# A decoder layer with 32 experts: the first two experts chosen from the counts of two token tiles, and another order of the experts

## The chip, the core and the metric

The kernel runs on one core of a Trainium2 chip. The metric is the device time of one execution in microseconds (us). TensorE is called PE, VectorE DVE, ScalarE ACT, GpSimd POOL and SyncE SP; SP issues nearly all transfers from HBM. "Tile" has three senses here, so they are kept apart: a *token tile* is 128 of the 512 tokens, a *weight tile* is one transfer of 1 MB of expert weights (1.0486 million bytes), and a *slot* is the SBUF buffer that a weight tile lands in.

## What is computed

One layer: an attention mixer, a layer norm, then 32 experts of which each token takes four, and a second layer norm. Cut to what matters:

```python
x = layer_norm(DN_ALPHA * x + mixed, ln1_g, ln1_b)            # 512 x 1024
logits = (xt @ w_router + b_router); top_logit, top_idx = lax.top_k(logits, 4)
gates = softmax(top_logit)
# for each expert e, over the tokens that chose it:
h = xb @ w_gate_up[e] + b_gate_up[e]                          # 1024 -> 2048
act = (clip(up, -7, 7) + 1) * (min(gate, 7) * sigmoid(1.702 * gate))
y = act @ w_down[e] + b_down[e]                               # 1024 -> 1024
out[token] += gate_of(token, e) * y
x = layer_norm(DN_ALPHA * x + out, ln2_g, ln2_b)
```

Everything is float32. An expert's weights are 12 MB, 8 weight tiles of gate/up and 4 of down; all 32 are read, 402.7 million bytes.

## The kernel before

**Attention** works by token tile, in the order 0, 3, 1, 2 (`ORDER`); `PLAN` starts one head's scores per step and carries out one task of a finished token tile in between: `mix_all`, `out_proj` twice, `norm`, `logits`, `logits2`, `ranks`. `route` picks the four experts of each token, `rank` counts for each token its place among the tokens of its expert. After the last token tile `counts` adds up the tokens per expert, and `order_experts` sorts the experts into the *positions* of `KINDS`, the largest counts into the roomiest kinds.

**Kinds.** A position of kind H has 128 places and multiplies in three passes of split weights: ACT writes the high part (L251), DVE the low part (L252), into *hi/lo rooms* (three `whi`, three `wlo` of 1 MB each). Kind L has 64 places and T has 32; both take the raw float32 weights as they landed, with 2 or 4 row groups of PE at a time (L1377). G is H and T at once, D is H and L at once. A slot comes free when an H tile has been split, or when the last matmul on a raw tile is done.

**The stream.** `Stream.ahead` (L153) issues weight tiles on SP in a fixed order whenever a slot is free: 11 slots (`NRAW`) during attention, some of them lent to q, k, v, 12 in the expert stage. `hold` stops it until `order_experts` is done, since until then no expert's number is known. Position 0 is an exception: it is always expert 0, so its 12 weight tiles can be fetched during attention (the `order` list brings its down tiles ahead of position 1's). The w_o weights sit split in the hi/lo rooms and two slots until the last `out_proj`.

**The first token rows.** While the last token tile is in hand, the rows of expert 0 from the other three are gathered (`prep2`, `gather`); the last token tile's rows come by matmuls with a selection (`first_xT`, L1270). In the stage itself PE runs gate/up of position b and then down of position b-1; `between(k)` prepares the next positions. At the end `tail` reads the outputs back and does the second layer norm.

Of the kernel before, what the change touches and what calls it, by code (L numbers as in the profile page):

```python
# [9 lines left out]
F32 = mybir.dt.float32  # L10
F32R = mybir.dt.float32r
BF = mybir.dt.bfloat16
# [30 lines left out]
KINDS = "HTLHLLGLTHLHLLDLTHLHHTHLHLHHHLLL"  # L43
# [6 lines left out]
assert len(KINDS) == E and KINDS[:2] == "HT" and KINDS[-3:] == "LLL"  # L50
# [47 lines left out]
def constants():  # L98
# [30 lines left out]
    by_room = [0] + sorted(range(1, E), key=lambda b: -CAP[KINDS[b]])  # L129
# [4 lines left out]
    put("keys", np.broadcast_to(np.where(np.arange(E) < 1, 2.0 ** 21, 0) + E - 1 - np.arange(E), (P, E)))  # L134
# [5 lines left out]
class Stream:  # L140


    def __init__(self, kn):
        self.kn, self.src, self.raw, self.cv = kn, [], {}, {}
        self.nd = self.nc = self.at = 0

        self.order, self.hold = None, 1 << 30
# [5 lines left out]
    def ahead(self, most=None):  # L153
        kn = self.kn
        while self.nd < min(len(self.src), self.hold) and kn.used < kn.limit and (most is None or self.nd <= most):
            i = self.order[self.nd] if self.order else self.nd
# [51 lines left out]
class Kernel:  # L208
# [14 lines left out]
    def raw_slot(self, dt=F32):  # L223

        j = self.free.pop(0)
# [4 lines left out]
    def release(self, *tiles):  # L230
        for t in tiles:
            j, = [j for j, s in self.slots.items() if s is t]
            del self.slots[j]
            self.free.append(j)

    def release_all(self):
        self.slots, self.free = {}, list(range(self.nslots))
# [64 lines left out]
    def setup(self, ctx):  # L302
# [32 lines left out]

        order = list(range(len(self.st.src)))
        order[n0 + 8:n0 + 20] = order[n0 + 16:n0 + 20] + order[n0 + 8:n0 + 16]
        self.st.order, self.st.hold = order, n0 + 12
# [254 lines left out]
    def attention(self):  # L593
        nc, tc, i = self.nc, self.tc, self.i
        with ExitStack() as cx:
# [157 lines left out]
            ranked = []  # L753

            def norm(q):
# [6 lines left out]
                if len(ranked) == NT - 1:  # L762
                    self.xT0 = [sc.tile([P, 512], F32, name="xT0", tag="sc") for _ in range(2)]
                    self.first_xT(self.xg[0], self.ident, True)

            def logits(q):
# [19 lines left out]
                nc.sync.dma_start(self.x1d[q * P:(q + 1) * P], z)  # L786
# [8 lines left out]

            def ranks(q):
                self.rank(q)
                ranked.append(q)
                if len(ranked) < NT:
                    self.places(q)  # L800
                    self.prep_tile((0, 0), q)
                else:
                    mf = w.tile([P, P], F32, name="mf1", tag="pT", bufs=3)
                    nc.vector.tensor_scalar(mf, self.iob, self.rk1[:, q, 0:1], None, op0=ALU.is_equal)
                    ps = self.counts()
                    x1 = state.pop((q, "z"))
                    self.first_xT(x1, mf, False, range(4))
# [969 lines left out]
```

## Time and profile before

| | |
|---|---|
| median of 3 runs | 1383.42 us (1383.14 to 1383.57) |
| the profiled execution | 1382.91 us, of which the span of instructions 1381.0 |
| mean granted TensorE clock | 0.967 of full speed |
| PE / DVE / ACT / POOL busy | 91% / 53% / 40% / 12% |
| moved by DMA | 464.69 MB, on average 336 GB/s |
| chain that ended last, by engine | PE 43%, DMA 39%, DVE 8% |

The profile's page cuts the span into 40 slices of 34.5 us; attention and routing are the first nine or so, the expert stage the rest. A matmul's busy time is longer than its spacing, since matmuls are pipelined. Times in the views count from the first instruction.

### The profile page before, as it was taken

The page shows a single profiled execution, that of the slowest core. Times are in us where ns is not written, and L with a number is a line of the kernel's source. Part 1 is how long each engine was busy: PE and PEld are TensorE (multiplying, and loading weights), DVE is VectorE, ACT ScalarE, POOL GpSimd, SP SyncE. Part 2 cuts the span into 40 slices and gives each one's busy share as a digit, 9 for nine tenths or more (in the row PEclk, how much of TensorE's full clock was granted, in tenths as well). Part 3 has the DMA queues.
Part 4 walks back from the last instruction along what each step waited for, and adds up shares of the span by engine and source line. Part 5 has one row for each costly group of instructions (what it writes and reads, how often), then busy time and mean ns, then how long its engine had stood idle before and what let it go on. Part 6 is the DMA issues. An engine that isn't in the chain of part 4 may idle for free.

```text
span 1381.0 us, 17825 instructions
## 1 busy us (share of the span) xinstructions
PE 1256.8 (91%) x6424; PEld 804.6 (58%) x6424; DVE 734.4 (53%) x1280; ACT 559.2 (40%) x828; POOL 160.4 (12%) x180
## 2 busy tenths in 40 slices
PE   6989698978999899998999999999998999999972
PEld 5768597866564354555544445477574657875320
DVE  4553555458563254356434336288565567973155
ACT  3432543324352143335234235267444365753201
POOL 2232100011010000101000001010010110000004
PEclk9999899887999999999999999999999999999987
DMA  9201641348999999999999999999999999999981
GB/s 331 86 1 61 240 146 62 122 157 298 374 418 420 419 419 419 417 419 418 421 418 420 363 394 386 418 419 418 420 418 419 419 419 409 418 387 419 415 363 71
DMA packets 76331, 464.69 MB, mean 336 GB/s; under 512 B 10306, under 2 KB 11506, under 8 KB 26064
## 3 DMA queue, kind: packets, MB, share of 16 engines
q1 hardware_dynamic: 65824, 435.42, 77.3%
q0 software_dynamic: 7840, 18.66, 3.7%
q10 hardware_dynamic: 2576, 9.44, 1.9%
q8 instruction: 52, 0.85, 0.2%
q14 instruction: 39, 0.32, 0.1%
HBM read 445.60 MB, written 25.03 MB: 341 GB/s over the span
## 4 chain that ended last, share of the span: by engine, by line
PE 43%; DMA 39%; DVE 8%; ACT 3%; POOL 2%; issue 2%; ACTq 0%; SPq 0%; POOLq 0%; DVEq 0%
DMA raw<-in_w_gate_up_dram 23%; DMA raw<-in_w_down_dram 12%; PE acc L1377 10%; PE acc L258 6%; PE acc L259 6%; PE acc L260 6%; DVE wlo L252 3%; DMA yr<-yd 1%; DMA raw<-yd 1%; PE ip L258 1%; PE ip L260 1%; PE ip L259 1%; PE zp L260 1%; PE zp L258 1%; PE zp L259 1%
## 5 line engine op out<-in xcount | busy, mean ns | idle before, releaser
L252 DVE TENSOR_TENSOR wlo<-raw,whi 128x1024 fp32r<-128x1024 f32 (+3 forms) x361 | 422.1, 1222 | 136.3 <-ACT whi L251 133.6
L251 ACT CAST whi<-raw 128x1024 fp32r<-128x1024 f32 (+3 forms) x361 | 358.7, 1046 | 167.7 <-DMA raw<-in_w_down_dram 78.2
L1377 PE MATMUL acc<-raw,xTs 128*64 128x512 f32 (+1 forms) x1280 | 264.0, 600 | 11.7 <-DMA raw<-in_w_gate_up_dram 11.3
L258 PE MATMUL acc<-whi,xTh 128*128 128x512 f32 x448 | 182.8, 408 | 4.5 <-issue 3.9
L259 PE MATMUL acc<-wlo,xTh 128*128 128x512 f32 x448 | 177.9, 397 | 0.9 <-DVE wlo L252 0.9
L260 PE MATMUL acc<-whi,xTl 128*128 128x512 f32 x448 | 177.8, 397 | 0.0
L1377 PEld LDWEIGHTS acc<-raw,xTs 128*64 128x64 f32 (+1 forms) x1280 | 70.0, 129 | 146.0 <-issue 110.2
L1488 POOL DMA_INDIRECT yd<-y,idx x34 | 50.6, 1489 | 658.5 <-ACT y L1477 470.8
L1377 PE MATMUL acc<-raw,aTs 128*64 128x512 f32 (+1 forms) x704 | 115.5, 521 | 0.1
L1427 DVE TENSOR_SCALAR u<-acc 128x512 f32<-128x512 f32 (+1 forms) x48 | 31.8, 662 | 148.3 <-ACT s L1426 148.3
L258 PEld LDWEIGHTS acc<-whi,xTh 128*128 128x128 f32 x448 | 84.8, 189 | 36.4 <-issue 12.8
L259 PE MATMUL acc<-wlo,aTh 128*128 128x512 f32 x224 | 90.5, 404 | 13.6 <-DVE wlo L252 13.6
L259 PEld LDWEIGHTS acc<-wlo,xTh 128*128 128x128 f32 x448 | 84.8, 189 | 21.1 <-DVE wlo L252 2.7
L260 PEld LDWEIGHTS acc<-whi,xTl 128*128 128x128 f32 x448 | 84.7, 189 | 20.5
L258 PE MATMUL acc<-whi,aTh 128*128 128x512 f32 x224 | 90.1, 402 | 2.3 <-ACT whi L251 2.3
L1426 ACT ACTIVATE s<-acc 128x512 f32<-128x512 f32 (+1 forms) x48 | 27.5, 574 | 156.6 <-PE acc L1370 82.4
L260 PE MATMUL acc<-whi,aTl 128*128 128x512 f32 x224 | 88.8, 396 | 0.0
L1377 PEld LDWEIGHTS acc<-raw,aTs 128*64 128x64 f32 (+1 forms) x704 | 39.4, 128 | 66.8 <-issue 58.8
L1333 DVE SCALAR_TENSOR_TENSOR aTl<-tp,aTh 128x512 fp32r<-128x512 f32 x28 | 18.0, 686 | 106.6 <-ACT aTh L1329 106.6
L1305 POOL DMA_INDIRECT xg<-x1d,idx x34 | 40.3, 1185 | 294.5 <-issue 211.8
L1477 ACT COPY y<-acc 128x1024 f32<-128x1024 f32 (+2 forms) x32 | 23.6, 738 | 115.8 <-PE acc L260 61.4
L259 PEld LDWEIGHTS acc<-wlo,aTh 128*128 128x128 f32 x224 | 42.2, 188 | 29.5 <-DVE wlo L252 20.4
(333 smaller groups left out, 1533.6 us busy)
## 6 DMA issues: line engine op xcount, KB each, us to landing
raw<-in_w_gate_up_dram SPq DMA_DIRECT2D x256, 1024.0 KB, 20.4
raw<-in_w_down_dram SPq DMA_DIRECT2D x128, 1024.0 KB, 20.8
yd<-xg ACTq DMA_DIRECT2D x4, 2048.0 KB, 7.7
raw<-in_w_in_dram SPq DMA_DIRECT2D x6, 1024.0 KB, 15.1
raw<-yd SPq DMA_DIRECT2D x5, 1024.0 KB, 19.9
raw<-in_w_o_dram SPq DMA_DIRECT2D x4, 1024.0 KB, 5.0
yr<-yd SPq DMA_DIRECT2D x3, 1024.0 KB, 19.9
raw<-in_x_dram SPq DMA_DIRECT2D x4, 512.0 KB, 10.1
```

The costliest lines, as they stand in the source:

```text
L251: nc.scalar.copy(hi[:, js], t[:, js])
L252: nc.vector.tensor_tensor(lo[:, js], t[:, js], hi[:, js].bitcast(F32), op=ALU.subtract)
L258: nc.tensor.matmul(out, l[0], r[0], start=start, stop=False)
L259: nc.tensor.matmul(out, l[0], r[1], start=False, stop=False)
L260: nc.tensor.matmul(out, l[1], r[0], start=False, stop=stop)
L1305: nc.gpsimd.indirect_dma_start(out=B["xg"], out_offset=None, in_=self.rows(self.x1d, n), in_offset=bass.IndirectOffsetOnAxis(ap=B["idx"][: ...
L1333: nc.vector.scalar_tensor_tensor(lo, v, scale, hi.bitcast(F32), op0=ALU.mult, op1=ALU.subtract)
L1377: self.nc.tensor.matmul(o[n * i:n * i + n], lT, r, start=start, stop=stop)
L1426: nc.scalar.activation(s, ps[:, :w], AF.Silu, scale=SW)
L1427: nc.vector.tensor_scalar(u, ps[:, w:2 * w], LIM + 1.0, 1.0 - LIM, op0=ALU.min, op1=ALU.max)
L1477: nc.scalar.copy(y, B["d"])
L1488: self.nc.gpsimd.indirect_dma_start(out=self.rows(self.yd, n), out_offset=bass.IndirectOffsetOnAxis(ap=B["idx"][:, 1:2], axis=0), in_=y, i ...
```

## The change

1. **Two experts picked early.** When two token tiles are routed (0 and 3), `pick_first` takes the two experts with the fewest tokens so far; `keys` later forces them to positions 0 and 1. Both positions are now kind T. Their 16 gate/up tiles and the first one's down tiles (`hold = n0 + 20`) may then be issued; the experts' numbers are read by SP into registers. Nothing is fetched before that.
2. **Raw weights in rooms of split ones.** After w_o's last use the rooms that held it are taken by five weight tiles of position 1 (`extra`) and by the expert biases (`bias_early`, which now loads both).
3. **The last token tile's chain** is written out in `last_two`: the mixing of the last tile stands between the routing steps of the one before, no weights are split there, and the rows of the first expert for the last two token tiles come by matmuls of 32 columns (`first_rows`, `first_more`).
4. **Another order of positions**: 11 H and 15 L instead of 12 and 14; T, G and D as many as before.

```diff
-KINDS = "HTLHLLGLTHLHLLDLTHLHHTHLHLHHHLLL"
+KINDS = "TTLHHHLLLGTLDTLHHLLHLHLHHLLHHLLL"
...
     def ahead(self, most=None):
...
+            if kn.used >= kn.limit and not kn.extra:
+                break
...
     def raw_slot(self, dt=F32):
+        if self.extra:
+            tag = self.extra.pop(0)
+            t = self.hp.tile([P, 2048], dt, name="raw", tag=tag)
...
-        order[n0 + 8:n0 + 20] = order[n0 + 16:n0 + 20] + order[n0 + 8:n0 + 16]
-        self.st.order, self.st.hold = order, n0 + 12
+        self.n0 = self.st.hold = n0
...
             def ranks(q):
                 self.rank(q)
                 ranked.append(q)
-                if len(ranked) < NT:
-                    self.places(q)
-                    self.prep_tile((0, 0), q)
...
+                self.places(q)
+                self.route2(q)
+                if len(ranked) == 2:
+                    self.pick_first(ranked)
+                    self.st.hold = self.n0 + 20
                     self.st.ahead()
+                    B = self.blk[0, 0] = {}
+                    self.at0 = self.columns(B, 0, w)
+                    for t in ranked:
+                        self.prep_tile((0, 0), t)
                     self.prep2((0, 0), ranked)
                     self.gather((0, 0))
+            def last_two(p, q):
+                flush()
+                logits2(p)
+                mix_t(q, 1)
+                out_half(q, 1, 0)
+                self.rank(p)
+                ranked.append(p)
+                self.places(p)
+                mp = first_col(p)
+                self.route2(p)
+                out_proj(q, 0)
+                out_proj(q, 1)
+                for j in range(4):
+                    self.st.cv.pop(wo0 + j)
+                self.release(*self.in_ring)
+                self.bias_early(nc.scalar)
+                self.extra = ["whi", "wlo", "whi", "wlo", "whi"]
+                self.st.ahead()
+                flush()
+                norm(q)
+                self.xT0 = sc.tile([P, 512], F32, name="xT0", tag="sc")
+                self.first_rows(self.xg[0])
+                self.first_more(state.pop((p, "z")), mp, False)
+                logits(q)
+                logits2(q)
+                self.rank(q)
+                ranked.append(q)
+                ps = self.counts()
+                mq = first_col(q)
+                self.first_more(state.pop((q, "z")), mq, True)
+                self.order_experts(ps)
+                self.st.hold = len(self.st.src)
+                self.st.ahead()
+                self.places(q)
...
+    def pick_first(self, tiles):
+        ps = self.tp()
+        for j, t in enumerate(tiles):
+            nc.tensor.matmul(ps[:, :E], self.oneb, self.sel[:, t], start=j == 0, stop=j == len(tiles) - 1)
+        few = sm.tile([P, E], F32, name="few", tag="lg")
+        nc.vector.scalar_tensor_tensor(few, ps[:, :E], -float(E), self.c["iotae"], op0=ALU.mult, op1=ALU.add)
+        nc.vector.max(mx, few)
+        nc.vector.max_index(ix, mx, few)
+        nc.vector.tensor_copy(self.idf, ix[:, :2])
+        nc.vector.tensor_copy(self.ids, self.idf[:1])
...
+    def first_more(self, rows, mf, last):
+        for k in range(KD):
+            c = k % 2 * P + k // 2 * 32
+            self.nc.tensor.matmul(self.xT0[:, c:c + 32], rows[:, k * P:(k + 1) * P], mf, start=False,
+                                  stop=last and k == KD - 1)
```

The order of instructions shows the change at three places. On SP, from the write of the second token tile's rows (`x1d`) on; `z` is a token tile's input rows, `raw` a weight tile. Before:

```order
L786 DMA x1d<-z 128x1024
L710 DMA z<-in_x_dram 128x1024
L163 DMA raw_2173<-in_w_gate_up_dram 128x2048
L163 DMA raw_2175<-in_w_gate_up_dram 128x2048
L163 DMA raw_2177<-in_w_gate_up_dram 128x2048
L786 DMA x1d<-z 128x1024
L163 DMA raw_2331<-in_w_gate_up_dram 128x2048
L163 DMA raw_2333<-in_w_gate_up_dram 128x2048
L163 DMA raw_2335<-in_w_down_dram 128x2048
L710 DMA z<-in_x_dram 128x1024
L786 DMA x1d<-z 128x1024
```

and in the changed kernel:

```order
L788 DMA x1d<-z 128x1024
L1611 TENSOR_LOAD ids
L1611 ISA x2
L165 ISA
L165 DMA raw_2088<-in_w_gate_up_dram 128x2048
L165 ISA
L165 DMA raw_2099<-in_w_gate_up_dram 128x2048
L165 ISA
L165 DMA raw_2101<-in_w_gate_up_dram 128x2048
L715 DMA z<-in_x_dram 128x1024 x2
L165 ISA
L165 DMA raw_2222<-in_w_gate_up_dram 128x2048
```

Three weight tiles had been issued before these rows; now the load of the two numbers (`ids`) and the first three weight tiles stand ahead of the `z` loads, which both come here. After the next `x1d` write three more weight tiles follow, then the five in the rooms and two in w_o's slots.

On PE, from the rank of token tile 3 (`utb`) on, before:

```order
L996 MATMUL tp<-sel,utb 128x32
L684 MATMUL po<-raw_804,pT 128x128
L684 MATMUL po<-raw_807,pT 128x128
L684 MATMUL po<-raw_810,pT 128x128
L684 MATMUL po<-raw_474,pT 128x128
```

and in the changed kernel:

```order
L1020 MATMUL tp<-sel,utb 128x32
L1211 LDWEIGHTS oneb
L1211 MATMUL tp<-sel,oneb 128x32
L1211 LDWEIGHTS oneb
L1211 MATMUL tp<-sel,oneb 128x32
L1356 LDWEIGHTS m
L1356 MATMUL tp<-orh,m 128x4
L1356 LDWEIGHTS m
L1356 MATMUL tp<-orh,m 128x4
L689 MATMUL po<-raw_804,pT 128x128
```

The matmuls of the pick (L1211) and of the first expert's row numbers (L1356, which need DVE's `m`) now stand ahead of attention's.

On PE after the router logits of token tile 1 (`x1T`), before:

```order
L792 MATMUL tp<-wr,x1T 128x32 x8
L995 LDWEIGHTS oneb
L995 MATMUL tp<-sel,oneb 128x32
L995 LDWEIGHTS oneb
L995 MATMUL tp<-sel,oneb 128x32
L996 LDWEIGHTS utb
L996 MATMUL tp<-sel,utb 128x32
L1280 LDWEIGHTS m
L1280 MATMUL tp<-rh,m 128x4
```

and in the changed kernel:

```order
L794 MATMUL tp<-wr,x1T 128x32 x8
L722 MATMUL tp<-cst,mix 128x128 x4
L266 MATMUL zp<-whi,mh 128x512
L267 MATMUL zp<-wlo,mh 128x512
L268 MATMUL zp<-whi,ml 128x512
```

Twelve output-projection matmuls of token tile 2 (`zp`) now follow at once, then the rank of token tile 1, then the other 24; the three matmuls on `m` (L1280) are gone from here.

## Rows read from the trace of the kernel before

**Rows 1.** The page, 40 slices of the span: GB/s moved.
```profile
GB/s 331 86 1 61 240 146 62 122 157 298 374 418 420 419 419 419 417 419 418 421 418 420 363 394 386 418 419 418 420 418 419 419 419 409 418 387 419 415 363 71
```

**Rows 2.** Busy time by stretch: us, engines' busy us (instructions), clock, DMA share, GB/s.
```profile
280.00:300.00 20.00, 16.13 (x85) 13.21 (x84) 9.29 (x27) 2.58 (x6) 2.84 (x3) 0.83 0.57 222
300.00:320.00 20.00, 11.60 (x75) 10.15 (x73) 15.33 (x45) 7.44 (x14) 1.70 (x2) 0.74 0.51 188
320.00:340.00 20.00, 18.60 (x77) 14.30 (x78) 16.86 (x42) 11.18 (x15) 4.53 (x7) 0.83 0.79 275
340.00:360.00 20.00, 19.18 (x142) 11.18 (x140) 13.62 (x30) 9.46 (x13) 3.06 (x3) 1.00 0.85 330
360.00:380.00 20.00, 20.00 (x92) 12.06 (x92) 8.78 (x17) 6.51 (x9) 1.02 (x1) 1.00 1.02 419
...
770.00:790.00 20.00, 20.00 (x87) 9.40 (x89) 5.13 (x12) 2.28 (x4) 0.00 (x0) 1.00 0.84 331
820.00:840.00 20.00, 20.00 (x139) 9.25 (x139) 1.45 (x6) 3.43 (x6) 1.20 (x2) 1.00 0.85 321
1230.00:1250.00 20.00, 20.00 (x97) 10.69 (x97) 8.28 (x17) 7.50 (x9) 2.31 (x2) 1.00 0.92 366
```

**Rows 3.** Timeline of SP's issues: start us, us until the last, what, count.
```profile
263.38 1.29 SPq L163 DMA_DIRECT2D raw<-in_w_gate_up_dram  x3
...
285.00 1.21 SPq L163 DMA_DIRECT2D raw<-in_w_gate_up_dram  x2
286.26 0.49 SPq L163 DMA_DIRECT2D raw<-in_w_down_dram  x1
286.79 0.56 SPq L710 DMA_DIRECT2D z<-in_x_dram  x1
...
307.50 2.52 SPq L163 DMA_DIRECT2D raw<-in_w_down_dram  x3
318.92 42.02 SPq L163 DMA_DIRECT2D raw<-in_w_gate_up_dram  x16
```

**Rows 4.** Timeline of PE from 255 to 322 us; in brackets the idle time before.
```profile
255.02 0.18 PE L996 MATMUL tp<-sel,utb 128*128 128x32 bf16 x1
...
287.93 0.18 PE L996 MATMUL tp<-sel,utb 128*128 128x32 bf16 x1 [1.76 <-DVE sel L987]
...
289.38 0.19 PE L1280 MATMUL tp<-rh,m 128*128 128x4 bf16 x1 [1.24 <-DVE m L1246]
...
292.22 0.63 PE L260 MATMUL zp<-whi,ml 128*128 128x512 f32 x1
...
301.86 1.95 PE L1270 MATMUL xT<-cst,xg 128*128 128x128 f32 x16
...
321.40 0.76 PE L258 MATMUL acc<-whi,xTh 128*128 128x512 f32 x1 [3.86 <-issue]
```

**Rows 5.** Timeline of DVE, the same columns.
```profile
257.58 0.23 DVE L983 TENSOR_SCALAR gates<-gates,gs 128x4 f32<-128x4 f32 x1
...
270.34 0.69 DVE L747 SCALAR_TENSOR_TENSOR z<-z,zp 128x512 f32<-128x512 f32 x1 [0.16 <-PE zp L260]
...
298.01 0.69 DVE L747 SCALAR_TENSOR_TENSOR z<-z,zp 128x512 f32<-128x512 f32 x1 [6.14 <-DMA z<-in_x_dram]
...
307.17 3.70 DVE L252 TENSOR_TENSOR wlo<-raw,whi 128x512 fp32r<-128x512 f32 x6
...
315.93 0.17 DVE L1138 CAST vi<-v 1x32 int32<-1x32 f32 x1
...
325.32 0.29 DVE L1160 TENSOR_TENSOR otmp<-rk,oat 128x128 f32<-128x128 f32 x1
```

**Rows 6.** Matmul groups of a gate/up half: a T position, then an L position.
```profile
L1377 PE MATMUL acc<-raw,xTs 128*32 128x512 f32 x64 | 7.5, 597 | 0.0
...
L1377 PE MATMUL acc<-raw,xTs 128*64 128x512 f32 x64 | 14.6, 597 | 0.0
```

**Rows 7.** SP's waits between 765 and 860 us: total us, times, longest.
```profile
SPq L163 <- PE acc L1377: 55.2, 26, 5.8
```

More of the change, by code (lines that the diff above doesn't have):

```diff
@@ L233, in release @@
             del self.slots[j]
-            self.free.append(j)
+            if isinstance(j, int):
+                self.free.append(j)
     def release_all(self):
-        self.slots, self.free = {}, list(range(self.nslots))
+        self.slots, self.free, self.extra = {}, list(range(self.nslots)), []
     def convert(self, t, a, n, in_ring):
@@ L1032, in moe @@
         self.oh = mp.tile([P, 2, E], F32, name="oh")
-        xT = self.blk[0, 0]["xT"] = self.pair("xT")
-        for g in range(2):
-            self.split([x[:, 4 * g:4 * g + 4] for x in xT], self.xT0[g].rearrange("p (k t) -> p k t", k=4))
+        xT = mp.tile([P, 2, 4, 32], F32, name="xTs", tag="xTh")
+        nc.scalar.copy(xT, self.xT0[:, :256].rearrange("p (k h s) -> p k h s", k=2, h=4))
         self.rest()
+        self.bias_part(0)
         self.scx.close()
@@ new lines, in second_between @@
+        def second_between(k):
+            if k == 0:
+                next(perm)
+                self.prep_sel(1)
+            elif k == 1:
+                next(perm)
+                self.bias_part(1)
+            elif k == 2:
+                for _ in perm:
+                    pass
+                self.prep((2, 0))
+            elif k == 3:
+                self.prep2((2, 0))
+                self.gather((2, 0))
+            elif k == 4:
+                self.prep((3, 0))
+            elif k == 5:
+                self.load_aT(0)
+            elif k == 6:
+                self.prep2((3, 0))
+                self.gather((3, 0))
@@ L1265, in prep_sel, with first_rows @@
                 self.nc.vector.tensor_scalar(B["sel"][j], self.oneb, oh[j], None, op0=ALU.mult)
-    def first_xT(self, rows, mf, start, ks=range(KD)):
-        for k in ks:
-            self.nc.tensor.matmul(self.xT0[k // 4][:, k % 4 * P:(k % 4 + 1) * P], rows[:, k * P:(k + 1) * P], mf,
-                                  start=start and k % 4 == 0, stop=not start and k % 4 == 3)
+    def first_rows(self, rows):
+        for k in range(2):
+            self.nc.tensor.matmul(self.xT0[:, k * P:(k + 1) * P], rows[:, k * P:(k + 1) * P], self.ident,
+                                  start=k == 0, stop=False)
+    def first_more(self, rows, mf, last):
[3 more added lines that the diff above has]
+                                  stop=last and k == KD - 1)
     def prep2(self, u, tiles=range(NT)):
```

211 lines of the change are left out of this document (100 added, 111 removed).

## The prediction

> **What bounds the kernel now.** I read the page's slices first. From the twelfth slice on the transfers move 409 to 421 GB/s nearly throughout, until the last two; the eleven before move less, most of them far less [rows 1]. So the expert stage is a stream that can't go faster, about 419 GB/s or 2.50 us per weight tile of 1.0486 MB, and its end is set by two things: how many bytes have moved when the stream begins to flow, and how many are lost when it stops. Three places later on fall short, slices 23 to 25 and 36 [rows 1].
>
> I then read stretches, to price the shortfalls [rows 2]. From 300 to 360 us they are 419 - 188, 419 - 275 and 419 - 330 GB/s over 20 us each: 464 x 20 us = 9.28 MB. In the stage, 770 to 790 us lacks 88 x 20 us = 1.76 MB, 820 to 840 us 1.96 MB, 1230 to 1250 us 1.06 MB. PE is busy all through the last three: there the stream stops because all slots are full, and SP waits for PE's matmuls on raw tiles, 55.2 us in 26 waits [rows 7]. The first two lie at the D position, the third behind the three H in a row at positions 26 to 28.
>
> Why the start is slow: SP's issues are sparse. Three weight tiles have gone before those rows, six more by 286.7 us, three at 307.5; the thirteenth goes at 318.92 us, and the following sixteen take 42.0 us, since each waits for a slot [rows 3]. Between 287 and 307 us there is no free slot that may be filled, after 307 no expert that may be fetched. PE starts the experts at 321.40 us [rows 4], with an H position, which gives a slot back only as fast as splitting runs.
>
> Order on PE before that: logits of token tile 1, a wait of 1.76 us for the selection and 1.24 us for `m`, then 36 output-projection matmuls, which begin at half clock, 1.2 GHz (0.63 us for a matmul), and end near 302 us, where the row matmuls begin [rows 4].
>
> **The change, part by part.**
>
> *The pick (a new wait).* After the rank of token tile 3, PE has the matmuls on `m` ahead of attention's. DVE must first finish the gates, at 257.81 us [rows 5], then 17 small operations: the pick, the keys, the columns, two `m`. Such operations take 0.16 to 0.29 us [rows 5]; at 0.22 that is 3.8 us, so `m` is there near 261.6. PE, free at 255.20 [rows 4], idles 6.4 us; everything behind it on PE (scores, values, output projection of tile 1) and on DVE moves by that. The wait is new in kind; its ends are 3 us (DVE interleaves) and 10 us. I also charge 3 us for the clock: after the 1.8 and 1.2 us waits at 288 us the granted clock was 0.83 of full in that stretch, so 17% of 20 us was lost [rows 2], and an idle spell of 6 us will not do better.
>
> *SP.* The two numbers are ready near 258.7, and SP had its first weight tile out 2.8 us after `vi` was written [rows 3, 5], so the first three tiles go at about 261.5 to 263.5. The three tiles fetched earlier than that before are no loss: the engines are nearly idle there. The `z` loads now stand behind three weight tiles. In the same position `z` of tile 2 was issued at 286.79 and arrived after 298.01 [rows 3, 5], 11.2 us; that puts `z` of tile 1 at 275, and DVE took it at 270.34 before [rows 5] and now comes 6.4 us later, near 277. I price it at nothing; without that cover it costs up to 4 us. The second three tiles follow as before, the third three wait behind the `x1d` write of tile 1 and go near 293 instead of 285.
>
> *The last tiles.* The waits of 1.76 and 1.24 us and the 3.4 us of lower clock go, because twelve matmuls of tile 2 stand there: 6.4 us, just what the pick costs. The projection so ends at 302 + 3 (clock) = 305. Behind it, DVE's splitting of 3.70 us no longer stands before the logits (2.9 us of it were in their way), and the 3.86 us before the first expert matmul shrink to one copy [rows 4, 5]: the experts start near 321.4 + 3 - 2.9 - 3 = 318.5.
>
> *The rooms (the main gain).* Counting from 293 us: three tiles and an `x1d` write, three tiles into rooms whose last use is over near 299, biases of 0.8 MB, two tiles in rooms and two in slots from 305, one in the twelfth slot: 11 tiles and 1.3 MB, 12.8 MB or 31 us of transfers. That reaches to 324, and slots come back from 319.5 on, one per 0.94 us, since a T half has 7.5 us of matmuls on 8 tiles [rows 6], against 2.50 us per transfer. So the flow is unbroken from 293 us. It wins the 9.28 MB of 300 to 360 us, and trails at 300 by 8 us of what moved there before (222 GB/s [rows 2]: 1.78 MB). Sum 7.5 MB / 0.419 = **17.9 us**. The ends: 22.1 us if the third group isn't late; 9.6 us if the flow only begins at 315 (15 x 231 GB/s = 3.5 MB less). Reading the numbers into registers costs SP under 1 us per tile beside 2.50 us of transfer: nothing.
>
> The Trainium skill speaks against this sum: "DMA: Bandwidth & Descriptors", Specifications, gives about 358 GB/s as the HBM limit of one core. By it the missing bytes would be (170 + 83 + 28) x 20 us = 5.6 MB, and the term about (5.6 - 1.8) / 0.358 = 11 us. The row of 360 to 380 us shows 419 GB/s, so the measurement decides and the rule gets no chance here.
>
> *The order of positions.* At D, PE takes an H and an L tile from each weight tile and falls behind. Before, an L follows (14.6 us for its 8 tiles), now a T (7.5 us) [rows 6]: PE is 7 us sooner at D's down tiles, more than the second stop lasted. I let the first stop stay and count the second as gone, 1.96 / 0.419 = 4.7 us. The stop behind three H goes, as only two stand before the last three L: 2.5 us. Three H now stand at positions 3 to 5, behind a start with full slots; for this I take back 1 us (ends 0 and 5). Term **6.2 us**, ends -2.5 (nothing won, a stop like the one at 1230 added) and 11.4 (all three stops gone).
>
> *Bytes.* One H less for an L: its gather and its scatter halve, 2 x 0.26 MB = **1.3 us**. The biases' extra 0.5 MB inside the flow cancel the `z` that left it. The fourth token tile's splitting of weights that went off ACT and DVE was not in the end's way beyond the 2.9 us above.
>
> Sum: 17.9 + 6.2 + 1.3 = 25.4 us. The profiled execution took 1382.91, its span 1381.0; the median is 0.5 us above it. 1383.4 - 25.4 = **1358 us**.
>
> **The rivals.**
> - *The hand-over is late.* The pick's idle time, a low clock after it and the `z` loads add up, the projection ends ten microseconds later, and with it the rooms. For it: PE has no idle time to give between 255 and 276. Against it: the flow has some 5 us to spare before the first slot returns. Start term 9.6: 9.6 + 6.2 + 1.3 = 17, 1366 us.
> - *The order moves the stops.* Both stops at D stay and the H, H, H behind the full start adds one: order term -2.5. 17.9 - 2.5 + 1.3 = 16.7, 1367 us.
> - *Better on all points:* no late group and no stop, 22.1 + 11.4 + 1.3 = 34.8, 1349 us.
> - *Slower: overflow.* The picked experts were chosen by half of the tokens and have 32 places. From the 33rd token of either on, the loop behind the tail runs a whole expert, 12 tiles at 2.50 us = 30 us, and reads outputs and inputs of the norm again, some 10 MB or 25 us: at least 55 us, 1413 us. Against it: routed on the reference's own inputs the two least chosen have 12 and 13 tokens in tiles 0 and 3, and 15 and 17 in all.
> - *It doesn't do what it says:* rooms or slots come back no sooner, and SP issues the 13th tile at 319 as before: 1383 us. The order on SP speaks against it.
>
> **How the numbers follow.** Forecast 0.60 (1352 to 1364 on its own), late hand-over 0.20, order 0.08, better 0.08, slower 0.02, no effect 0.02. About 0.2%, 2.8 us, is what a measurement of this kernel can tell from no change. Faster: 0.96 less a tail of the late hand-over, 0.95; within 0.2%: 0.02; slower 0.03, with that tail. The range runs from inside the better case, 1346, over the two cases near 1367 to 1370; about 0.1 stays outside.
>
> **What would show it.** Right: 17 weight tiles issued before PE's first expert matmul; that matmul before 324 us; over 400 GB/s in every 20 us from 300 on; one stop at D instead of two, none near the end; an idle spell of PE of about 6 us behind the rank of token tile 3. Wrong: a stretch under 350 GB/s between 300 and 360 us, stops behind the first three H, or a tail that is longer than before, since nothing here touches it.

## The result, and the profile after

The changed kernel took **1359.41 us** (median of 4 runs, 1357.27 to 1361.93), the kernel before 1383.28 beside it (4 runs, 1378.21 to 1383.57): ratio 0.9837, 95% interval 0.9805 to 0.9868. The forecast was 1358. The profiled execution took 1357.27 us, its span is 1355.4.

From the page of the changed kernel, the speed by slices and the bytes, against [rows 1]:

```profile
GB/s 327 98 1 62 231 100 32 177 225 409 416 419 420 418 420 420 420 415 419 419 372 419 419 418 419 419 420 419 419 418 418 417 417 409 415 419 415 395 363 73
DMA packets 76411, 465.28 MB, mean 343 GB/s; under 512 B 10176, under 2 KB 11376, under 8 KB 26144
```

The stream reaches over 400 GB/s two slices of 34 us earlier than before (in the 10th instead of the 12th), slices 23 to 25 no longer fall short, and up to the last three a single slice, the 21st, does. The bytes grew by 0.6 MB (464.69 before).

Stretches, with the columns of [rows 2]:

```profile
300.00:320.00 20.00, 12.72 (x67) 9.15 (x66) 8.44 (x38) 4.25 (x8) 1.38 (x2) 0.66 1.02 360
320.00:340.00 20.00, 16.66 (x125) 5.13 (x125) 12.44 (x58) 1.55 (x4) 1.59 (x2) 0.83 1.01 419
340.00:360.00 20.00, 17.29 (x168) 7.06 (x166) 2.54 (x13) 2.12 (x5) 3.68 (x5) 1.00 1.01 415
360.00:380.00 20.00, 19.86 (x146) 10.99 (x143) 11.25 (x22) 9.84 (x12) 2.85 (x2) 1.00 1.01 418
690.00:710.00 20.00, 20.00 (x99) 8.56 (x99) 5.20 (x12) 2.65 (x5) 0.99 (x1) 1.00 0.89 346
...
770.00:790.00 20.00, 20.00 (x97) 13.77 (x97) 14.86 (x19) 11.43 (x14) 1.28 (x1) 1.00 1.01 418
820.00:840.00 20.00, 20.00 (x97) 10.97 (x97) 8.47 (x16) 6.55 (x8) 2.68 (x2) 1.00 1.02 422
1230.00:1250.00 20.00, 20.00 (x90) 8.86 (x90) 1.59 (x4) 1.61 (x2) 0.99 (x1) 1.00 1.01 417
1250.00:1270.00 20.00, 18.36 (x86) 6.23 (x82) 4.09 (x16) 3.44 (x6) 0.97 (x1) 1.00 0.98 376
```

The 20 us from 300, 320 and 340 us move 360, 419 and 415 GB/s where they moved 188, 275 and 330. The places of the old stops run full (418, 422, 417). One stop is left at D, now at 690 to 710 us (346 GB/s), since the order moved D, and at 1250 us the stream falls short once more (376).

SP's issues (start, us until the last of the group, what, count), against [rows 3]:

```profile
254.97 1.52 SPq L165 DMA_DIRECT2D raw<-in_w_gate_up_dram  x3
256.59 0.99 SPq L715 DMA_DIRECT2D z<-in_x_dram  x2
266.54 1.75 SPq L165 DMA_DIRECT2D raw<-in_w_gate_up_dram  x3
287.44 0.33 SPq L788 DMA_DIRECT2D x1d<-z  x1
288.03 21.80 SPq L165 DMA_DIRECT2D raw<-in_w_gate_up_dram  x10
314.71 11.04 SPq L165 DMA_DIRECT2D raw<-in_w_down_dram  x4
```

Three tiles, two `z` loads, three tiles, then nothing for 19 us but the wait for `x1d` of the last but one token tile; ten tiles from 288 on, of which four go by 291.4, the fifth at 299.8 and the sixth at 306.2; then one at a time, as slots come back. PE, against [rows 4] (in brackets the idle time before an instruction and what ended it):

```profile
256.37 0.35 PE L1356 MATMUL tp<-orh,m 128*128 128x4 bf16 x2 [5.94 <-DVE m L1315]
...
297.75 0.60 PE L1339 MATMUL xT<-cst,xg 128*128 128x128 f32 x4
...
304.56 3.62 PE L794 MATMUL tp<-wr,x1T 128*128 128x32 f32 x16 [2.79 <-ACT x1T L783]
...
315.08 3.35 PE L1450 MATMUL acc<-raw,xTs 128*32 128x512 f32 x16
```

The wait at the pick (first row), the end of the projection (the row matmuls of L1339 follow it), the wait of the last logits (L794) for ACT, and the first expert matmul (L1450) at 315.08, 6.3 us earlier than before (most of these 6.3 are taken off below).

**One thing has to be taken off before these are compared.** Some runs of the changed kernel get through the first 205 us up to 4 us earlier than others, and the profiled execution above is one of those. The write of the first finished token tile to `x1d` shows it (of three such writes the durations in ns, then the first and the last start). Before, after, and the changed kernel once more (run e1_same):

```profile
L786 SPq DMA_DIRECT2D x1d<-z x3: 326/326/327, 208.9 to 284.6; - x3
```
```profile
L788 SPq DMA_DIRECT2D x1d<-z x3: 326/331/339, 204.9 to 287.4; - x3
```
```profile
L788 SPq DMA_DIRECT2D x1d<-z x3: 327/332/339, 208.7 to 292.4; - x3
```

208.9 and 208.7 are of one kind, 204.9 is not. So like is compared with like below: "early" stands for a profile with that write near 205 (204.9 to 205.8 in four profiles), "late" for one near 208 to 209 (207.8 to 208.9 in ten). Late against late the change is worth 1382.91 - 1361.75 = 21.2 us, and 4.5 us of the difference between the profiles before and after are this. Medians mix both kinds; four to six runs of each kernel leave them 2 to 4 us uncertain.

### The profile page after: what moved, and what is told of

Its sections match the earlier page's. It is cut to its first block, busy times and chain, and to the rows that moved or that the text cites. A ratio compares the mean times of both kernels' runs of the same rounds, so it can differ in the third digit from the quotient of the medians.

```text
span 1355.4 us, 17704 instructions
## 1 busy us (share of the span) xinstructions
PE 1239.3 (91%) x6376; PEld 784.1 (58%) x6376; DVE 708.5 (52%) x1279; ACT 534.1 (39%) x795; POOL 154.7 (11%) x177
## 3 DMA queue, kind: packets, MB, share of 16 engines
q0 software_dynamic: 7584, 18.47, 3.7%
q10 hardware_dynamic: 3056, 10.75, 2.1%
HBM read 445.33 MB, written 25.30 MB: 347 GB/s over the span
## 4 chain that ended last, share of the span: by engine, by line
PE 52%; DMA 31%; DVE 7%; ACT 3%; POOL 2%; issue 1%; ACTq 0%; SPq 0%; POOLq 0%; DVEq 0%
DMA raw<-in_w_gate_up_dram 19%; PE acc L1450 13%; DMA raw<-in_w_down_dram 8%; PE acc L266 8%; PE acc L267 8%; PE acc L268 8%; DVE wlo L260 2%; DMA yr<-yd 1%; DMA raw<-yd 1%; PE ip L266 1%; PE ip L268 1%; PE ip L267 1%; PE po L689 1%; PE zp L268 1%; PE zp L266 1%
## 5 line engine op out<-in xcount | busy, mean ns | idle before, releaser
L260 DVE TENSOR_TENSOR wlo<-raw,whi 128x1024 fp32r<-128x1024 f32 (+3 forms) x331 | 393.7, 1238 | 108.8 <-ACT whi L259 105.6
L259 ACT CAST whi<-raw 128x1024 fp32r<-128x1024 f32 (+3 forms) x331 | 335.1, 1063 | 139.7 <-DMA raw<-in_w_gate_up_dram 48.3
L1450 PE MATMUL acc<-raw,xTs 128*64 128x512 f32 (+1 forms) x1344 | 286.4, 621 | 11.5 <-DMA raw<-in_w_gate_up_dram 10.1
L266 PE MATMUL acc<-whi,xTh 128*128 128x512 f32 x416 | 167.8, 403 | 1.8 <-ACT whi L259 1.6
L267 PE MATMUL acc<-wlo,xTh 128*128 128x512 f32 x416 | 164.0, 394 | 3.1 <-DVE wlo L260 3.0
L1450 PEld LDWEIGHTS acc<-raw,xTs 128*64 128x64 f32 (+1 forms) x1344 | 75.7, 133 | 154.9 <-issue 126.9
L268 PE MATMUL acc<-whi,xTl 128*128 128x512 f32 x416 | 163.7, 393 | 0.0
L1450 PE MATMUL acc<-raw,aTs 128*64 128x512 f32 (+1 forms) x736 | 122.6, 526 | 1.9 <-DMA raw<-in_w_down_dram 1.9
L267 PE MATMUL acc<-wlo,aTh 128*128 128x512 f32 x208 | 81.9, 394 | 4.3 <-DVE wlo L260 4.3
L1450 PEld LDWEIGHTS acc<-raw,aTs 128*64 128x64 f32 (+1 forms) x736 | 41.2, 129 | 73.5 <-issue 61.4
L266 PE MATMUL acc<-whi,aTh 128*128 128x512 f32 x208 | 82.4, 396 | 0.5 <-ACT whi L259 0.5
L1550 ACT COPY y<-acc 128x512 f32<-128x512 f32 (+2 forms) x32 | 23.2, 725 | 120.8 <-PE acc L268 72.5
```

The costliest lines, as they stand in the source:

```text
L259: nc.scalar.copy(hi[:, js], t[:, js])
L260: nc.vector.tensor_tensor(lo[:, js], t[:, js], hi[:, js].bitcast(F32), op=ALU.subtract)
L266: nc.tensor.matmul(out, l[0], r[0], start=start, stop=False)
L267: nc.tensor.matmul(out, l[0], r[1], start=False, stop=False)
L268: nc.tensor.matmul(out, l[1], r[0], start=False, stop=stop)
L1450: self.nc.tensor.matmul(o[n * i:n * i + n], lT, r, start=start, stop=stop)
```

## Experiments

Each ran beside the kernel before. e1 to e4, e5 to e8 and e9 to e12 shared a chip each, on which the medians of before were 1381.88, 1382.66 and 1383.06; across chips the ratios to before are what compares.

### e1: the changed kernel again

No edit.

> The changed kernel again, to see its two groups of times (1357 and 1362 us). My theory: the attention stage, whose code is not changed, ends 4 to 5 us earlier or later by the phase in which TensorE's clock falls, and that alone makes the groups; so some runs of the kernel before should be near 1378 and some near 1383, and the difference between the same groups 20 to 23 us. The rival: the spread is the change's own (its transfers collide differently); then the kernel before stays within 1 us and the changed one does not.

1360.86 us (5 runs: 1357.28, 1358.04, 1360.86, 1361.75, 1362.14), ratio 0.9841 (0.9825 to 0.9857). Two single values near 1357.5 and three near 1361.5; the profiled one is late. Its stretches:

```profile
0.00:240.00 240.00, 201.19 (x1117) 173.70 (x1117) 121.01 (x309) 96.44 (x235) 46.34 (x79) 0.96 0.34 120
240.00:280.00 40.00, 31.46 (x178) 29.29 (x179) 19.07 (x68) 12.68 (x40) 4.02 (x7) 0.70 0.49 192
280.00:300.00 20.00, 19.81 (x121) 17.06 (x120) 9.85 (x28) 3.76 (x8) 1.69 (x2) 1.00 0.38 142
300.00:320.00 20.00, 14.77 (x87) 13.21 (x89) 9.54 (x31) 1.45 (x3) 1.69 (x2) 0.67 1.02 366
320.00:340.00 20.00, 15.42 (x116) 4.51 (x112) 12.19 (x59) 4.36 (x9) 1.11 (x1) 0.82 1.01 419
340.00:360.00 20.00, 17.68 (x168) 7.09 (x164) 4.65 (x23) 1.74 (x4) 4.16 (x5) 0.91 1.02 416
360.00:380.00 20.00, 20.00 (x152) 9.06 (x147) 7.56 (x16) 6.56 (x10) 1.39 (x2) 1.00 1.01 417
```

Adding up GB/s times us to 380 us: 28.8 + 7.7 + 2.8 + 7.3 + 8.4 + 8.3 + 8.3 = 71.6 MB here; the kernel before, by [rows 2] and its 133 GB/s up to 240 us and 144 from there to 300, 31.9 + 8.6 + 3.8 + 5.5 + 6.6 + 8.4 = 64.8; the early profile after, the same way (120 and 207 GB/s in those two), 73.4. The bytes lost in stops later (419 GB/s x 920 us from 380 to 1300 us, less what moved) are 5.7 MB before, 3.4 here and 3.3 in the early profile. Bytes ahead at 380 us, plus stops saved, less the 0.6 MB that grew, over 0.419: (6.8 + 2.3 - 0.6) / 0.419 = 20.3 us, where the two profiled times differ by 21.2. The same sum gives each of the other profiled runs to 1.3 us. The two kinds of runs are there again, and the kernel before spreads over the same 5 us beside them (11 runs, 1378.33 to 1383.48), so the rival, a spread of the change's own, falls.

That TensorE's clock alone makes the kinds, as my theory had it, the traces do not show. From 40 to 60 us the granted clock is 0.91 in all ten late profiles and 1.00 in all four early ones. But e1 is behind the early profile after before that: SP issues the first w_o tile at 29.26 us in e1 and at 28.03 in the early one, so 1.2 of the 3.8 us arise ahead of that stretch.

### e2: the old order on the new start

```diff
-KINDS = "TTLHHHLLLGTLDTLHHLLHLHLHHLLHHLLL"
+KINDS = "TTLHLLGLTHLHLLDLTHLHHLHLHLHHHLLL"
```

> The early pick, the rooms and the last chain stay; behind the first three positions (T, T, L) the order of before returns (D followed by an L, three H in a row near the end), with the same number of each kind. My theory: the stops of the stream at D (about 7 to 8 us in two places) and behind the three H (2 to 3 us) return, 10 to 11 us instead of the 6 us that the changed kernel loses: 4 to 6 us slower than the changed kernel, about 1363 to 1366 us. The rival, that the early start alone wins and the stops only follow from it: within 1.5 us of the changed kernel.

1362.82 us (4 runs), ratio 0.9868 (0.9852 to 0.9885). The profiled run is early, 1362.63, so it stands against 1357.27: 5.4 us. (The medians of e1 and e2 differ by 2.0 us only, but mix early and late runs.) The stops of the old order are back, each some 20 us earlier than in [rows 2]:

```profile
750.00:770.00 20.00, 20.00 (x89) 9.44 (x89) 5.13 (x12) 2.28 (x4) 0.00 (x0) 1.00 0.82 317
...
800.00:820.00 20.00, 20.00 (x139) 9.35 (x137) 0.93 (x5) 2.91 (x5) 1.00 (x1) 1.00 0.86 321
...
1210.00:1230.00 20.00, 20.00 (x96) 10.78 (x96) 8.77 (x17) 7.71 (x9) 2.29 (x2) 1.00 0.94 375
```

Lost from 380 to 1300 us: 5.8 MB, after the change 3.3; 2.5 MB / 0.419 = 6.0 us. By 380 us 73.5 MB have moved, as in the profile after. So the order term is 5.4 to 6.0 us, and the rival falls.

### e3: no rooms

```diff
-                self.extra = ["whi", "wlo", "whi", "wlo", "whi"]
+                self.extra = []
```

> The five weight tiles in the rooms of the split w_o are left out, so at most 11 weight tiles (12 with the late slot) are on the way before TensorE starts the experts. My theory: the stream is out of slots from about 310 us until the first release near 316 us and then waits for each release of the first two experts; 5 tiles of 2.5 us less whatever fits in later, so 7 to 13 us slower than the changed kernel. The rival, that the T positions give slots back so fast that the rooms are worth little: 0 to 3 us.

1368.59 us (6 runs), ratio 0.9911 (0.9892 to 0.993). The profiled run, early, took 1364.86, 7.6 us over 1357.27 (0.9 us of it stand at the first `x1d` write already, 205.8 against 204.9), though its first expert matmul came earlier, at 313.35. Its stretches:

```profile
300.00:320.00 20.00, 12.78 (x75) 8.86 (x74) 10.95 (x43) 4.25 (x8) 1.69 (x2) 0.63 0.79 267
320.00:340.00 20.00, 18.41 (x146) 5.89 (x150) 11.11 (x57) 1.93 (x5) 2.11 (x2) 0.86 0.89 348
```

Against 360 and 419 that is (93 + 71) x 20 us = 3.3 MB or 7.8 us. My theory held, the rival falls: five tiles weigh 5.2 MB or 12.5 us, and some 7 of it show in the time.

### e4: the biases off ACT's queue

Seen in the timeline of ACT after the change (the last column as for PE; ACTq rows are issues):

```profile
294.70 1.91 ACTq L1283 DMA_DIRECT2D braw<-in_b_gate_up_dram  x3
296.65 7.17 ACTq L1283 DMA_DIRECT2D braw<-in_b_down_dram  x4
303.92 1.07 ACT L783 COPY x1T<-tp 128x512 f32<-128x512 f32 x2 [9.64 <-DMA braw<-in_b_gate_up_dram]
```

The four issues of `b_down` take ACT until 303.82, 7.17 us, and the copy that the last logits need goes only then. I had not foreseen this, and SP's wait lists name the bias transfer too, 5.8 us.

```diff
-                self.bias_early(nc.scalar)
                 self.extra = ["whi", "wlo", "whi", "wlo", "whi"]
...
                 logits(q)
+                self.bias_early(nc.gpsimd)
                 logits2(q)
```

> The eight small transfers of the expert biases go from ACT's queue (ahead of the weight tiles in the rooms) to POOL's, behind the last normalisation. In the changed kernel ACT stands still for them from 296.7 to 303.9 us, the transposed rows of the last token tile wait 2.8 us, and SP waits 5.8 us for one of them before a weight tile, so that 1.3 MB of flow are lost between 297 and 310 us. My theory: the flow is what counts, so this wins back 2 to 4 us. The rival, that the stream is bound by slots there and not by that wait: no difference (within 1 us), though the last token tile's chain ends 3 to 6 us earlier.

1361.79 us (5 runs), ratio 0.9852 (0.9839 to 0.9865): nothing gained. Profiles both late: 1361.91 and 1361.75. SP, then PE, then ACT:

```profile
293.00 11.39 SPq L165 DMA_DIRECT2D raw<-in_w_gate_up_dram  x10
318.85 8.30 SPq L165 DMA_DIRECT2D raw<-in_w_down_dram  x4
```
```profile
313.22 3.62 PE L1346 MATMUL xT<-mf,z 128*128 128x32 f32 x16 [0.69 <-DVE mf L804]
...
319.39 3.64 PE L1450 MATMUL acc<-raw,xTs 128*32 128x512 f32 x16 [2.12 <-DMA braw<-in_b_gate_up_dram]
```
```profile
318.96 0.37 ACT L1065 COPY xTs<-xT 128x256 f32<-128x256 f32 x1 [11.56 <-DMA braw<-in_b_down_dram]
```

The ten tiles go within 11.39 us instead of 20.89, the wait of the last logits is gone, and the first expert matmul is still at 319.39 (e1: 319.60): it now waits 2.12 us itself, with the bias transfers named. 300 to 320 us move 380 GB/s instead of 366, 320 to 340 us 407 instead of 419; by 340 us the sums are equal, 55.0 MB. SP, with all its slots in use, stood until 318.85. So the same number of tiles, only issued earlier, brought nothing while that matmul came no sooner. My theory fell, and the rival's number held. That the slots bind this does not show alone, since the edit put a wait in the place of the one it took away: PE is through with the matmuls of L1346 at 316.8 us, 2.3 us before e1, and ACT's copy of their result, which the first expert matmul needs, goes at 318.96, with one of the moved bias transfers named. What the kernel would take with the biases in neither place no run tried.

### e5: the pick's wait made smaller

```diff
-                    self.prep2((0, 0), ranked)
-                    self.gather((0, 0))
+                    pair = list(ranked)
+                    def first_gather():
+                        self.prep2((0, 0), pair)
+                        self.gather((0, 0))
+                    soon.append(first_gather)
...
                 convert()
+                while soon:
+                    soon.pop(0)()
```

> Edit: the one-hot rows and the gather of the first expert are written one step of the attention's plan later, so that PE's selection matmuls stand behind further attention work and their inputs are ready when PE comes to them; nothing is left out. My theory (the prediction's pick term): PE's wait of 5.9 us before the selection matmuls falls under 2 us, the half-clock stretch behind it goes or shrinks, everything behind it on PE comes 4 to 9 us earlier, the first expert matmul with it, and the kernel is 3 to 8 us faster than the changed kernel (1353 to 1358 where that reads 1361). Rival (the wait only takes up slack: PE would wait for the same DVE and ACT work later in the last chain): the wait goes and the first expert matmul still starts within 2 us of 319.5, the time within 2 us.

**1357.55 us** (5 runs, 1353.54 to 1358.3), ratio 0.982 (0.9798 to 0.9842). Profiled 1357.92, a late one: 3.8 us under e1, of which 0.9 stand at the first `x1d` write already (207.8, in e1 208.7).

```profile
259.75 0.34 PE L1362 MATMUL tp<-orh,m 128*128 128x4 bf16 x2 [3.10 <-DVE m L1321]
```
```profile
305.38 3.56 PE L794 MATMUL tp<-wr,x1T 128*128 128x32 f32 x16 [3.17 <-ACT x1T L783]
```

The wait shrinks to 3.10 us, not under 2: one step of the plan does not hold enough work to cover it. The last logits come at 305.38 instead of 309.06, the first expert matmul at 315.8 instead of 319.6, and 73.2 MB have moved by 380 us instead of 71.6: 1.6 MB / 0.419 = 3.8 us. Less the 0.9 that is 2.9 us, about what the wait lost (2.8) and just under my 3 to 8; by the ratios to before it is 2.9 too, though their intervals overlap. The granted clock from 240 to 280 us is 0.79 where e1 has 0.70; its part was not separated. The rival falls: the attention's chain has no slack, and what was taken from the pick's wait came back in full.

### e6 and e11: the last chain in the old order

```diff
                 flush()
                 logits2(p)
-                mix_t(q, 1)
-                out_half(q, 1, 0)
                 self.rank(p)
...
                 self.route2(p)
+                mix_t(q, 1)
+                out_half(q, 1, 0)
```

> Edit: in the last two token tiles' chain the rank, the places and the routing of the last but one token tile stand ahead of the last mix and its output half again, as the kernel before ordered them. My theory (the prediction: reordering wins back what the pick costs, 6.4 us): the wait of PE for the rank, which the mix covers now, stands open, the projection ends 4 to 7 us later (about 306 where the changed kernel has 300 to 302), and the time is 3 to 7 us over the changed kernel's. Rival (DVE and not PE sets the end of this chain, or the chain is covered by the weight stream): the projection ends later but the time is within 2 us.

1360.51 us (5 runs, 1356.26 to 1364.64), ratio 0.9845 (0.982 to 0.9871). Profiled 1363.75, late: 2.0 us over e1, while the ratios are alike (0.9841 for e1).

```profile
295.56 0.18 PE L1020 MATMUL tp<-sel,utb 128*128 128x32 bf16 x1 [1.76 <-DVE sel L1011]
...
308.57 1.38 PE L781 MATMUL tp<-cst,z 128*128 128x128 f32 x8 [0.39 <-DVE z L765]
...
320.80 3.31 PE L1450 MATMUL acc<-raw,xTs 128*32 128x512 f32 x16 [0.40 <-ACT xTs L1065]
```

The 1.76 us for the selection are back (first row), the last projection matmul starts at 305.6 instead of 302.5, but L794 no longer waits for ACT, since the bias issues are over by then, and the first expert matmul is 1.2 us later, not 3.2. 300 to 320 us move 305 GB/s instead of 366, 1.2 MB; by 380 us it is 1.1 MB or 2.6 us. Nearer to the rival than to my 3 to 7 us. Is the rest of the gain hidden behind the bias issues? e11 makes both edits, e4's and this one.

> Edit: two at once, the last chain in the old order and the bias loads on POOL's queue behind the last logits; to be read against the kernel with the bias loads alone. My theory (the reordering does win about 3 us at the projection's end, and the changed kernel loses them again since ACT stands behind the bias transfers): with the bias loads out of ACT's way the old order costs its full 3 us at the first expert matmul, and the time is 2 to 4 us over that of the kernel with the bias loads moved alone. Rival (what sets the first expert matmul is something else again, so that neither order is seen): first expert matmul and time within 1.5 us.

1361.5 us (5 runs), ratio 0.9834 (0.9814 to 0.9854); profiled 1362.26, late, against 1361.91 of e4. The first expert matmul did come later, at 321.82 (e4: 319.39), as my theory had it, and the time did not follow. The stretches from 300 and 320 us move 404 + 386 GB/s here, 380 + 407 in e4: the sums differ by 0.06 MB. What moved early enough to make up for the later slots I did not settle. So with the biases on POOL's queue the order of the last chain is worth nothing in time; with them on ACT's it is 2 us by one profile each and nothing by the ratios. My theory fell on the time.

### e7: the new order on the old start

The kernel before, with position 0 still H and position 1 still T:

```diff
-KINDS = "HTLHLLGLTHLHLLDLTHLHHTHLHLHHHLLL"
+KINDS = "HTLHHHLLLGTLDTLHHLLHLHLHHLLHHLLL"
```

> Edit: the kernel before, with its own start (first expert of 128 slots, then T), and only the order of kinds from the third position on as in the changed kernel. My theory (order term, 6.0 us by the lost bytes of the old order on the new start): the stop at 820 to 840 us and the one near 1240 go, the one at D stays, and the kernel is 4 to 7 us faster than before (1375 to 1378 where that reads 1382). Rival (three H right behind the first two positions fill the ring while the start's backlog is being worked off, on the old start with its later S above all): a stop appears between 330 and 450 us, and the gain is under 2 us or none.

**1376.83 us** (12 runs), ratio 0.996 (0.9947 to 0.9974), 5.5 us. Both profiles late: 1377.84 against 1382.91, 5.1 us. One stop at D, and two shortfalls near the end:

```profile
710.00:730.00 20.00, 20.00 (x100) 8.35 (x98) 5.20 (x12) 2.65 (x5) 1.01 (x1) 1.00 0.87 347
...
1230.00:1250.00 20.00, 20.00 (x97) 9.28 (x94) 10.25 (x13) 8.81 (x11) 2.04 (x2) 1.00 0.98 403
...
1270.00:1290.00 20.00, 20.00 (x95) 7.08 (x91) 4.09 (x16) 3.44 (x6) 0.99 (x1) 1.00 0.99 377
```

Between 380 and 700 us nothing falls short, so three H in a row behind the start cost nothing. Order and start add up: 5.5 us here, 5.4 to 6.0 in e2.

### e8: e5 and e4 together

> Edit: the pick's deferral and, besides, the bias loads moved from ACT's queue to POOL's behind the last logits. My theory (after the bias loads alone were worth nothing because the end of the chain was set elsewhere): with the pick's wait gone the chain's end comes earlier, and the bias loads still add nothing, within 2 us of the kernel with the pick deferred alone. Rival (the two are in series: with the first wait gone, ACT's block behind the bias transfers becomes the limit): 3 to 6 us faster than the pick's deferral alone.

**1356.96 us** (5 runs, 1354.26 to 1358.2), ratio 0.9818 (0.9796 to 0.9839), 0.6 us under e5. The first expert matmul comes at 313.86, 2.0 us before e5's, and 73.9 MB are moved by 380 us (73.2). My theory held within what can be told; against the rival's 3 to 6 us speak the profiles too (1356.96 and 1357.92, both late). As in e4 that matmul waits, 2.82 us, for ACT's copy, with a bias transfer named; so this weighs the loads on POOL's queue at that place, not a kernel without them in the way.

### e9, e10, e12: the changed kernel, one H behind D, three edits

e10 moves one H; e12 makes that edit, e4's, and e5's with two steps of delay instead of one.

```diff
-KINDS = "TTLHHHLLLGTLDTLHHLLHLHLHHLLHHLLL"
+KINDS = "TTLHHLLLGTLDTLHHLLHLHLHHLHLHHLLL"
```

> The changed kernel once more, as the measure for the three that run beside it on the same chip. Expected by all theories: 1357 to 1362 in single runs, ratio to before 0.982 to 0.986.

> Edit: one of the three H at positions 3 to 5 goes behind D, between the L at positions 25 and 26 (counted from 0, in the new order), nothing else. My theory (the stop at D comes from slots that are full there: the weight tiles that have landed and wait for PE grow by about 8 during D's 41 us, from about 3 to over 10 in a ring of 12; one H less ahead of D takes about 2 from that): the stop at 690 to 710 us goes or shrinks under 0.5 MB, no new one over 0.7 MB comes, and the kernel is 2 to 4 us faster than the changed one. Rival (PE's lag is only moved behind D): the stop near 1260 us grows, or a new one comes behind D, by what the first loses, and the time is within 1.5 us.

> Edit: three at once, the first expert's one-hot rows and gather two steps of the attention's plan later, the bias loads on POOL's queue behind the last logits, and the H moved behind D. My theory (they act at different places and add up): PE's wait at the pick under 1 us, the first expert matmul 4 to 6 us earlier at the same attention phase, no stop at D; 6 to 9 us faster than the changed kernel, 1351 to 1354. Rival (the earlier start brings the tiles in a bunch and the gain of the order is lost with it, or the later gather makes DVE late for the last tiles): not faster than the kernels with one edit, 1355 to 1358.

e9: 1361.72 us, ratio 0.9847 (0.9827 to 0.9866); profiled late, 1361.72.

e10: 1358.94 us (5 runs, 1357.58 to 1362.69), ratio 0.9827 (0.9813 to 0.984); profiled late, 1362.69. The stop was not smaller, only earlier:

```profile
660.00:680.00 20.00, 20.00 (x87) 9.09 (x83) 5.20 (x12) 2.07 (x4) 0.00 (x0) 1.00 0.92 344
680.00:700.00 20.00, 19.07 (x137) 9.84 (x135) 12.72 (x20) 10.90 (x14) 2.38 (x2) 1.00 0.99 405
```

(75 + 14) x 20 us = 1.8 MB; e1 loses (19 + 71) x 20 us, the same, from 680 to 720 us. From 380 to 660 us PE waited 6.8 us in ten waits for weight tiles to land, in e9 3.4 us in six: ahead of D it already took tiles as they came, so an H less there made PE wait and not the lag smaller. My theory fell on the stop. The median is 2.8 us under e9's, with intervals that overlap and profiles that show no bytes for it; whether the time differs stays open.

e12: 1358.27 us (5 runs, 1354.02 to 1358.83), ratio 0.9817 (0.98 to 0.9834). Its profile is early, 1356.03 against 1357.27. PE's wait at the pick is 1.85 us, not under 1, the first expert matmul comes 2.7 us earlier (312.4), not 4 to 6, and another wait stands right behind the first now:

```profile
256.91 0.34 PE L1362 MATMUL tp<-orh,m 128*128 128x4 bf16 x2 [1.85 <-DVE m L1321]
258.57 1.22 PE L689 MATMUL po<-raw,pT 128*128 128x128 f32 x4 [1.32 <-ACT pT L678]
```

The stop at D is there too, earlier (349 GB/s from 650 to 670 us). The kernel is no better than e5 or e8: the rival. e5, e8 and e12 lie 3 to 4 us under the changed kernel on their chip or by the ratios, with intervals that overlap its own; e8 is the fastest, and one cannot tell it from the other two.

## Why the prediction was right, and where it was not

The direction, the range and the main mechanism held: 1359.41 in 1346 to 1370, faster by far more than 0.2%. Against the forecast's 25.4 us the like-for-like gain is 21.2, so **the sum was some 4 us too large**; that the median came within 1.4 us of 1358 is luck: of its four runs 1357.27 is early by its trace and 1357.52 probably, by its time, while the forecast was taken from a time of the late kind.

*Start term, 17.9 us: mis-sized by 2.2.* Late against late, 300 to 360 us won 178 + 144 + 86 GB/s x 20 us = 8.2 MB (predicted 9.28), and 280 to 300 us, at 142 GB/s where [rows 2] has 222, trailed by 1.6 MB (predicted 1.78): 6.6 MB, 15.7 us. The step that failed is "the flow is unbroken from 293 us": 300 to 320 us move 366 GB/s, not 419, 1.1 MB or 2.5 us short. SP was held between its fourth and sixth tile, with a landing weight tile and the bias transfer named; in e4, which freed it, the shortfall only moves behind 310 us, since the 16 tiles are then through before the first slot comes back. What the runs show to set the term is how many tiles may go ahead of the slots (e3: some 7 us for the five rooms) and when PE gets that far (e5: some 3 us). Untried is the end that I put at 22.1 us: SP still stands 19.4 us ahead of the second `x1d` write, and from 284 to 292 us e1 moves 2 GB/s.

*The steps behind it.* Late against late most fell where they were put: first tile at 259.3 (261.5), PE's wait at the pick 5.9 us until 260.7 (6.4, until 261.6), third group of tiles at 293.0 (293), projection through at 302.7 (305), first expert matmul at 319.6 (318.5). `z` behind three tiles cost nothing, as priced: DVE took it at 273.38 us, early profile, with no wait.

*The pick and the reordered chain, 6.4 and 3 for the clock against 6.4: near in size, in part argued.* Two rows of DVE, before and in e1, take the first half of tile 1's projection:

```profile
270.34 0.69 DVE L747 SCALAR_TENSOR_TENSOR z<-z,zp 128x512 f32<-128x512 f32 x1 [0.16 <-PE zp L260]
```
```profile
278.37 0.69 DVE L752 SCALAR_TENSOR_TENSOR z<-z,zp 128x512 f32<-128x512 f32 x1
```

By then e1 is 8.0 us behind (predicted 9.4): 5.9 of PE's wait, and about 2 beside a granted clock of 0.70 from 240 to 280 us, where it was 0.83. At the projection's end 0.9 us of it are left (301.9 and 302.7; predicted 3), so the chain behind won back 7.1 (6.4). e6, which puts back the order of the steps and neither the matmuls on `m` nor the splitting, loses 3.1 of these; the granted clock from 280 to 300 us is 1.00 in e1, 0.91 in e6 and was 0.83 before. That the rest is the clock is argued; no run took it apart.

*Unforeseen:* the bias issues on ACT, 7.17 us ahead of the last logits. Whether they cost time stays open: e4 moved them and won nothing, but another wait, with its own transfers named, then stood ahead of the first expert matmul.

*Order term, 6.2 us: right in sum*, 5.1 to 6.0 (e2, e7), less so in its parts. From 640 to 900 us, around D, 413 GB/s move where 404 did: 2.3 MB or 5.6 us, where the second stop had been put at 4.7. The stop for slots behind three H is gone as well: from 1200 to 1300 us SP waited 20.3 us for PE's matmuls on raw tiles before and 0.6 after. But its 2.5 us were not won, since another shortfall lies near its place; from 1180 to 1300 us 411 GB/s move where 408 did, 0.4 MB or 0.9 us. The prediction did not have it: at 1250 us SP issues the last norm's inputs,

```profile
1250.55 7.79 SPq L1664 DMA_DIRECT2D yr<-x1d  x4
```

the DMA engines are busy 0.98 of that stretch, and PE is not busy throughout. What those reads cost no run took apart; before, they go at 1275 us. The 1 us taken back for the H at the front was not needed.

*Bytes, 1.3 us: wrong.* They grew by 0.6 MB. A second token tile of zeros for `x1d`, 0.52 MB, stands in the diff (`sorted(...)[2:]` leaves two), and I overlooked it. The rest of what ACT's queue gained (9.44 to 10.75 MB) was moved to it, the last `x1d` write from SP and `b_down` from POOL's queue. Whether the gather and the scatter halved the counts leave open: HBM reads fell by 0.27 MB (445.60 to 445.33) and writes rose by 0.27 (25.03 to 25.30) instead of 0.52, as halving would have it, but POOL's queue, which carries both, lost 0.19 MB (18.66 to 18.47), less than the 0.26 of `b_down`. The zeros go at 138 us, during attention; the term was worth nothing.

*Signs named in advance:* 17 weight tiles issued before the first expert matmul: yes, 17. That matmul before 324: yes. One stop at D: yes; none near the end: no stop for slots, but the shortfall at 1250 us. Over 400 GB/s in every 20 us from 300 on: no, 360 in the first. An idle spell of 6 us at the pick: 5.94.

*The rivals.* The late hand-over did not come. Its size was nearly right: where attention alone is 4 us late, as in e1 against the profile after, 4.5 us are lost, so the 5 us that I gave the flow to spare do not exist. Stops were removed and not moved. The picked experts did not overflow: nothing longer stands behind the tail.

*The rule weighed.* The sum went by the measured 419 GB/s, and the stretches after the change run at 415 to 422 outside the stops. The Trainium skill's "HBM Reference", Specifications (TRN2), says that a core which streams alone gets about 425 GB/s and that some 358 is the share when both cores of a pair stream. This kernel runs on one core, so the trace agrees with that sentence; 358 was the wrong figure of that skill to hold against this sum.

## What to carry to other kernels

Where a stream runs at its ceiling, count bytes by a fixed time and bytes lost in stops: here these two numbers gave each profiled run to 1.3 us. The waits that e4 took from SP and from the last logits brought no time, as the first expert matmul came no sooner; look for the wait that takes a removed one's place before calling it free. What paid was more transfers ahead of the consumer (e3) and a whole chain that starts earlier, its first transfers included (e5). And before comparing two profiles look at a point ahead of every edit: 4 us of the difference between them were there.

## What the runs showed that I had not expected

Four issues of small bias transfers held ACT for 7.17 us (296.65 to 303.82 us), while the same four took 1.99 us on POOL's queue in e8 (from 303.96 us on); what held them on ACT was not tried. The same program gets through the first 205 us with 4 us of difference from run to run (204.9 and 208.7 in the rows above), and the late kind goes with a lower granted clock from 40 to 60 us; why a run is of one kind or the other stays open.
